# Retention input projection: seven block products in place of eight

## The chip, the cores and the metric

The kernel runs on one core of a Trainium2 chip. The metric is device time in microseconds. All arithmetic is float32; a float32 product is made of three matmuls on halves (a high part rounded to TensorE's fast float32 format and a low rest): high x high, low x high, high x low.

## The reference, cut to what matters

A trunk of two layers on 1024 tokens of width 1024: retention and an MLP, then chunked attention and an MLP. The change touches the first step, the projection of the normed input `hn` by the combined weight of retention (1024 x 6144: q 1024, k 1024, v 2048, gate 2048), and what is done at once with its four parts:

```python
hn = x * rsqrt(mean(x * x) + EPS) * mix_norm_g
proj = hn @ w_in                       # (1024, 6144)
q, k, v, g = split(proj)               # 4 heads: q, k 256 wide, v, g 512 wide
q, k = rope(q, pos), rope(k, pos) * RET_DK ** -0.5
# rope: t1*cos - t2*sin, t1*sin + t2*cos, for the two halves of 128 of each head
o = chunkwise retention of q, k, v with decay per head; then GroupNorm per head
y = silu(g) * o
h = x + y @ w_out
```

## The kernel before, in words

Engines: PE multiplies, DVE and ACT split and scale, POOL adds, SP issues most DMAs. The residual `h` lies transposed in SBUF: eight blocks `h[m]` of 128 features by 1024 tokens, worked on in two halves of 512 tokens (`hf`). Each token's 1/rms is kept as a row `rB`, equal on all partitions, and as columns `rcol`; it is applied after the products, which therefore start before the norm is known. `class Norm` (L185) makes the split operands of all sixteen (m, hf) pieces (`operand`) and the square sums (`square`, `sums`, `turn`).

The projection (L599 to L740) multiplies block by block. `xload` reads x in eight pieces of 512 KB, `xturn` turns each block by PE into PSUM, and operands and `h` are made from PSUM. `up_group` (L439) makes one PSUM bank of 128 columns by 512 tokens from 8 blocks x 3 matmuls. Queries and keys come in pairs of such banks: the rope (L644) takes four products by DVE and two adds by POOL with the tables `cosr`, `sinr` in SBUF, scaled once by `rB` (`rope_scale`), and stores to `qS`, `kS` in DRAM. The first group is multiplied while the second half of x is still being turned (L673 to L680). Values are made with tokens on partitions (`proj_tok`, L451: operands of x as weights, eight banks at once), scaled by ACT with `vsc` (decay times 1/rms) and stored to `vS`; the first half of head 0 stays in SBUF, already split (L703). Then the first queries and keys are loaded and split (L722 to L727), and the gate groups run: DVE scales, ACT does the SiLU, DVE the gain, and the store goes to `gS` (L728 to L740). Weights come 512 KB at a time (`wload`, two buffers) and are split by ACT and DVE.

The core of retention (L742) takes heads in turn: `score`, `turn_k`, `state`, `outs`, `gate`, with q, k, v and gate reloaded from DRAM through rings, and the output projection as filling work.

The other three large projections (both MLPs, attention input) already run a scheme with seven block products for eight (`XNorm` L266, `Group` L324, `Seven` L353). It is Strassen's scheme in Winograd's form: x is cut into 2 x 2 (even or odd feature blocks by token halves), the weight of 256 columns into 2 x 2 (even or odd feature blocks by column halves), and products 1, 2, 5, 6, 3, 7, 4 of four blocks x 3 matmuls are added into three PSUM banks A, B, C. Operands 1, 2 and 5, 6 (`EARLY`) are made before the stage, 3, 7, 4 (`late`) during it; `Group.sums` makes the weight sums on DVE, `make` splits a weight two products ahead (`AHEAD`). After product 2, 3, 7 and 4 one of the four results is complete, and the job's `done(z, hf, src)` finishes it (z: column half). The first two groups are interleaved, so that the late operands have time. Weights come 1 MB per group.

What sets the order: the program is built ahead of time; each engine and each DMA queue works through its own fixed list, which follows the program's order but lets later work whose inputs are expected move ahead. Tiles of one tag share `bufs` places; a new tile waits for the release of an old one, also where a closed pool's place is used again.

Of the kernel before, what the change touches and what calls it, by code (L numbers as in the profile page):

```python
# [76 lines left out]
def trunk_kernel(ctx: ExitStack, tc: tile.TileContext, I, out):  # L77
# [64 lines left out]
    plain = {}  # L142
# [25 lines left out]
    def tmp_tile(pl, name, dt=F32):  # L168
        return pl.tile([P, HT], dt, name=name, tag="tmp", bufs=9 if pl is plain.get("gp") else 5)
# [96 lines left out]
    class XNorm(Norm):  # L266
# [18 lines left out]
        def block(self, m, hf):  # L285
# [3 lines left out]
            if self.seen[j] < 4:  # L289
                return  # L290
# [3 lines left out]
            x.split(1, j, b11)  # L294
            nc.vector.scalar_tensor_tensor(out=t1, in0=b[0][1], scalar=g[0], in1=b11, op0=ALU.mult, op1=ALU.subtract)
            x.scaled(2, j, b[1][0], g[1])
# [4 lines left out]
        def late(self, xb):  # L301

            x, gp = self.x, self.gp
            x.add(xb, LATE)
# [19 lines left out]
    class Group:  # L324
# [9 lines left out]
        def sums(self, ws, products):  # L334
            a = self.a
            for p in products:
                self.s[p] = t = ws.tile([P, 4, P], F32, name="wS", tag="wS", bufs=4)
# [15 lines left out]
    class Seven:  # L353
# [4 lines left out]
        AHEAD, NORM = 2, 4  # L358

        def __init__(self, wa, jobs):  # L360
            self.wa, self.jobs, self.groups = wa, jobs, {}
            self.steps = ([(i, p) for i in range(2) for p in EARLY] + [(0, 3), (1, 3), (0, 7), (0, 4), (1, 7), (1, 4)]
                          + [(i, p) for i in range(2, len(jobs)) for p in SEVEN])
# [11 lines left out]
        def ready(self, s):  # L375
# [3 lines left out]
            if s == 0:  # L379
# [16 lines left out]
        def go(self, wr, psp, gp, x, hooks):  # L396
# [3 lines left out]
            for s, (i, p) in enumerate(self.steps):  # L400
# [20 lines left out]
                if s >= self.NORM:  # L421
# [4 lines left out]
    def spread(norm, xb, psp, more=()):  # L426
# [3 lines left out]
        for hf in range(2):  # L430
            hooks[2].append(lambda hf=hf: norm.sums(psp, hf))
            hooks[Seven.NORM].append(lambda hf=hf: norm.turn(psp, hf))
# [166 lines left out]
    rs = ctx.enter_context(ExitStack())  # L599
    rq = ctx.enter_context(ExitStack())  # L600
    plain["wp"] = pool(rs, "weightsR", RIGHT)
    with ExitStack() as ph:
        gp = pool(ph, "gemmA", LEFT)
        psp = pool(ph, "psA", None, 8, PSUM)
        norm = Norm(0, gp)
        with ExitStack() as st:
            rp = pool(st, "rope", RIGHT)
            xp = pool(st, "xin", RIGHT)
            cosr = rp.tile([P, S], F32, name="cosr")
            sinr = rp.tile([P, S], F32, name="sinr")  # L610

            def qk_src(i):
                hd, which = i // 2, i % 2
                c0 = which * D + hd * DK
                return [w_in[:, c0 + z * P:c0 + (z + 1) * P] for z in range(2)]

            def xload(hf, between=None):
                xs = []
                for c in range(4):
                    if c == 1 and between:  # L620
                        between()
                    xt = xp.tile([P, 4, 256], F32, name="xt", tag="xt", bufs=4)
                    DMA.dma_start(out=xt, in_=I["x"][0, hf * HT:(hf + 1) * HT, c * 256:(c + 1) * 256].rearrange("(t p) c -> p t c", p=P))
                    xs.append(xt)
                return xs

            def xturn(xs, hf, ms):
                for m in ms:
                    ps = psp.tile([P, HT], F32, name="ps", tag="ps")
                    for t in range(4):  # L630
                        nc.tensor.transpose(ps[:, t * P:(t + 1) * P], xs[m // 2][:, t, (m % 2) * P:(m % 2 + 1) * P], ident)
                    norm.operand(m, hf, ps)
# [5 lines left out]

            def rope_scale(hf):
                sl = slice(hf * HT, (hf + 1) * HT)  # L640
                for tb in (cosr, sinr):
                    nc.gpsimd.tensor_tensor(out=tb[:, sl], in0=tb[:, sl], in1=rB[:, sl], op=ALU.mult)

            def rope(i, hf, p1, p2):  # L644
                hd, dst = i // 2, (qS, kS)[i % 2]
                sl = slice(hf * HT, (hf + 1) * HT)
                a, b, c, d = (rp.tile([P, HT], F32, name=n, tag=n, bufs=2) for n in ("ra", "rb", "rc", "rd"))
                nc.vector.tensor_tensor(out=a, in0=p1, in1=cosr[:, sl], op=ALU.mult)
                nc.vector.tensor_tensor(out=b, in0=p2, in1=sinr[:, sl], op=ALU.mult)
                nc.vector.tensor_tensor(out=c, in0=p1, in1=sinr[:, sl], op=ALU.mult)  # L650
                nc.vector.tensor_tensor(out=d, in0=p2, in1=cosr[:, sl], op=ALU.mult)
                nc.gpsimd.tensor_tensor(out=a, in0=a, in1=b, op=ALU.subtract)
                nc.gpsimd.tensor_tensor(out=c, in0=c, in1=d, op=ALU.add)
                for d, t in enumerate((a, c)):
                    DMA.dma_start(out=dst[hd][d, :, sl], in_=t)

            turns = []
            xs0 = xload(0, lambda: turns.append(load_gains(psp, rp, [I["mix_norm_g"].rearrange("i (b p) -> (i b) p", p=P)], 0)))
            turns.pop()()
            raws = [wload(src, NB, P) for src in qk_src(0)]  # L660
            xs1 = xload(1)
            DMA.dma_start(out=cosr, in_=I["cos"])
            DMA.dma_start(out=sinr, in_=I["sin"])
            DMA.dma_start(out=odec, in_=I["odec"])
            DMA.dma_start(out=odec2, in_=I["odec2"])
            rest = load_gains(psp, rp, [I["mlp_norm_g"].rearrange("i (b p) -> (i b) p", p=P),
                                        I["final_norm_g"].rearrange("(b p) -> b p", p=P),
                                        I["ret_gn_g"][0].rearrange("(b p) -> b p", p=P)], 2 * NB)
            xturn(xs0, 0, range(4))
            ws = [wsplit(raws[0], NB, P, "act", "pool")]  # L670
            xturn(xs0, 0, range(4, NB))
            ws.append(wsplit(raws[1], NB, P, "act", "dve"))
            first = {0: [up_group(psp, norm, ws[0], 0)]}  # L673
            xturn(xs1, 1, range(NB))
# [3 lines left out]
            first[0].append(up_group(psp, norm, ws[1], 0))  # L678
            rest()
            first[1] = [up_group(psp, norm, w, 1) for w in ws]  # L680
            norm.sums(psp, 0)
            norm.sums(psp, 1)
            for i in range(1, 2 * RH):
                ws = [wunit(src, NB, P) for src in qk_src(i)]
                for hf in range(2):
                    p1, p2 = (up_group(psp, norm, w, hf) for w in ws)
                    if i == 1:
                        norm.turn(psp, hf)
                        rope_scale(hf)
                        rope(0, hf, *first[hf])  # L690
                    rope(i, hf, p1, p2)

        vdec = gp.tile([P, NB, RH], F32, name="vdec")
        DMA.dma_start(out=vdec, in_=I["vdec"])
        vsc = gp.tile([P, NB, RH], F32, name="vsc")
        for i in range(RH):
            nc.vector.tensor_tensor(out=vsc[:, :, i], in0=vdec[:, :, i], in1=rcol, op=ALU.mult)
        yp = pool(rs, "yR", RIGHT)
        vv = {}
        v0 = [yp.tile([P, 4, HT], F32R, name=n, tag=n, bufs=2) for n in ("yh", "yl")]  # L700
        for hd in range(RH):
            def evac(t, ps, hd=hd):
                if hd == 0 and t < 4:  # L703
                    hi, lo = vv[0, t] = tuple(z[:, t, :] for z in v0)
                    sc = vsc[:, t, 0:1]
                    nc.scalar.activation(hi, ps, AF.Copy, scale=sc)
                    nc.vector.scalar_tensor_tensor(out=lo, in0=ps, scalar=sc, in1=hi.bitcast(F32), op0=ALU.mult, op1=ALU.subtract)
                    return
                vt = tmp_tile(gp, "t")
                nc.scalar.activation(vt, ps, AF.Copy, scale=vsc[:, t, hd:hd + 1])  # L710
                DMA.dma_start(out=vS[hd][t * P:(t + 1) * P, :], in_=vt)
            proj_tok(psp, norm, w_in[:, 2 * D + hd * DV:2 * D + (hd + 1) * DV], evac)

        cq = pool(rq, "coreRqk", RIGHT)
        qk, kt, sc, stt = {}, {}, {}, {}
        maskt = cq.tile([P, RH, P], F32, name="maskt")
        DMA.dma_start(out=maskt, in_=I["mask"])

        def qk_tiles():
            return [cq.tile([P, 2, HT], F32R, name=n, tag=n, bufs=3) for n in ("qkh", "qkl")]  # L720

        for nm, src in (("q", qS), ("k", kS)):  # L722
            qk[0, nm, 0] = qk_tiles()
            for d in range(2):
                raw = tmp_tile(gp, "raw0")
                DMA.dma_start(out=raw, in_=src[0][d, :, 0:HT])
                split(raw, *(t[:, d, :] for t in qk[0, nm, 0]))  # L727
        def gate_evac(m, hf, ps):  # L728
            sl = slice(hf * HT, (hf + 1) * HT)
            t = tmp_tile(gp, "t")  # L730
# [588 lines left out]
```

## Time and profile before

| | us |
|---|---|
| runs | 2832.45, 2836.87, 2838.62 |
| median | 2836.87 |
| profiled execution | 2835.71 |
| its span, first to last instruction | 2833.9 |
| PE / DVE / ACT / POOL busy | 2751.2 / 1655.6 / 1080.2 / 170.2 |
| HBM read / written | 221.59 / 89.69 MB |

Busy time is the union of an engine's instructions. Matmuls are pipelined, so an instruction's duration is longer than the distance to the next; the distance is the price. The granted clock of PE has two levels, 1.2 and 2.4 GHz, and 1.00 means the higher one throughout. The projection takes the first fifth of the span; the MLPs' and the attention's projections lie at 895, 1563 and about 2150 us.

### The profile page before, as it was taken

To read this page: it belongs to the slowest core of one execution; us is meant where nothing else is said; L and a number is where in the kernel's file an instruction comes from. 1 tells how busy PE (TensorE), PEld (TensorE's weight loads), DVE (VectorE), ACT (ScalarE), POOL (GpSimd) and SP (SyncE) were. 2 spreads that over 40 slices of the span, in tenths; PEclk is the share of its full clock that TensorE was granted. 3 is DMA by queue.
4 is the path that set the end of the run, shared out by engine and by line. 5 is a ranking of instruction groups with operands and counts; after the bars stand their busy time and mean duration, and the time that the engine had idled before them with its cause. 6 is when DMAs were issued, how large, how long until landed. Compare 5 with 4: busy or idle time off the path is not lost.

```text
span 2833.9 us, 34421 instructions
## 1 busy us (share of the span) xinstructions
PE 2751.2 (97%) x12762; PEld 2262.3 (80%) x12762; DVE 1655.6 (58%) x2969; ACT 1080.2 (38%) x1930; POOL 170.2 (6%) x235
## 2 busy tenths in 40 slices
PE   8999999999999999999999999789989999999998
PEld 7888888878887788878888788578877888788887
DVE  5431123366658756554446867599988665644445
ACT  4001222243326444432123534387775444412222
POOL 1320000000000000000000000233320000000000
PEclk9999999999999999999999999899999999999999
DMA  4321333353210333252331455765512333433321
GB/s 146 105 96 60 112 107 98 99 172 112 82 60 27 117 114 110 93 169 89 97 100 45 113 193 156 198 166 151 151 50 71 104 110 114 147 96 99 112 86 60
DMA packets 246648, 310.92 MB, mean 110 GB/s; under 512 B 14568, under 2 KB 172368, under 8 KB 244432
## 3 DMA queue, kind: packets, MB, share of 16 engines
q1 hardware_dynamic: 244816, 304.46, 34.5%
q0 software_dynamic: 1536, 4.20, 0.5%
q8 instruction: 100, 1.64, 0.2%
q14 instruction: 68, 0.56, 0.1%
q10 hardware_dynamic: 128, 0.06, 0.0%
HBM read 221.59 MB, written 89.69 MB: 110 GB/s over the span
## 4 chain that ended last, share of the span: by engine, by line
PE 85%; DVE 8%; ACT 3%; DMA 2%; issue 1%; SPq 0%; POOL 0%; DVEq 0%; ACTq 0%
PE ps L166 18%; PE ps L164 18%; PE ps L165 18%; PE pA L164 6%; PE pA L166 5%; PE pA L165 5%; PE pC L164 3%; PE pC L166 3%; PE pC L165 3%; DVE pr L1151 1%; DVE ptl L140 1%; PE pB L164 1%; PE pB L166 1%; PE pB L165 1%; PE po L1187 1%
## 5 line engine op out<-in xcount | busy, mean ns | idle before, releaser
L491 DVE TENSOR_TENSOR h<-ps,h 128x512 f32<-128x512 f32 x352 | 242.4, 689 | 339.4 <-PE ps L166 338.9
L136 ACT CAST whi<-wraw 128x1024 fp32r<-128x1024 f32 x132 | 139.0, 1053 | 769.9 <-PE ps L165 601.6
L165 PE MATMUL ps<-ul,whi 128*128 128x512 f32 x960 | 374.0, 390 | 1.9 <-DVE ul L140 1.7
L166 PE MATMUL ps<-uh,wlo 128*128 128x512 f32 x960 | 373.5, 389 | 0.0
L164 PE MATMUL ps<-uh,whi 128*128 128x512 f32 x960 | 373.0, 389 | 0.0
L166 PE MATMUL pA<-xh,wl 128*128 128x512 f32 x704 | 277.2, 395 | 10.0 <-DVE wl L140 10.0
L164 PE MATMUL pA<-xh,wh 128*128 128x512 f32 x704 | 278.3, 400 | 3.4 <-DVE c L417 2.7
L165 PE MATMUL pA<-xl,wh 128*128 128x512 f32 x704 | 278.2, 395 | 0.0
L140 DVE TENSOR_TENSOR wlo<-wraw,whi 128x1024 fp32r<-128x1024 f32 x131 | 165.0, 1260 | 165.4 <-ACT whi L136 165.3
L165 PEld LDWEIGHTS ps<-ul,whi 128*128 128x128 f32 x960 | 180.2, 188 | 41.2 <-DVE ul L140 3.6
L164 PEld LDWEIGHTS ps<-uh,whi 128*128 128x128 f32 x960 | 180.1, 188 | 37.6 <-ACT uh L136 0.4
L166 PEld LDWEIGHTS ps<-uh,wlo 128*128 128x128 f32 x960 | 180.2, 188 | 37.1
L164 PE MATMUL ps<-hhi,whi 128*128 128x512 f32 x512 | 202.8, 396 | 2.2 <-ACT whi L136 1.4
L165 PE MATMUL ps<-hlo,whi 128*128 128x512 f32 x512 | 202.3, 395 | 0.0
L166 PE MATMUL ps<-hhi,wlo 128*128 128x512 f32 x512 | 202.3, 395 | 0.0
L164 PEld LDWEIGHTS pA<-xh,wh 128*128 128x128 f32 x704 | 133.4, 190 | 43.2 <-DVE c L417 13.6
L166 PEld LDWEIGHTS pA<-xh,wl 128*128 128x128 f32 x704 | 133.6, 190 | 41.2 <-DVE wl L140 12.7
L165 PEld LDWEIGHTS pA<-xl,wh 128*128 128x128 f32 x704 | 133.5, 190 | 27.1
L136 ACT CAST wh<-wS 128x512 fp32r<-128x512 f32 x176 | 109.0, 621 | 116.0 <-PE pB L165 59.1
L164 PE MATMUL pC<-xh,wh 128*128 128x512 f32 x352 | 139.1, 395 | 3.3 <-ACT wh L136 2.1
L166 PE MATMUL pC<-xh,wl 128*128 128x512 f32 x352 | 138.6, 394 | 1.0 <-DVE wl L140 1.0
L165 PE MATMUL pC<-xl,wh 128*128 128x512 f32 x352 | 138.6, 394 | 0.0
(243 smaller groups left out, 5528.0 us busy)
## 6 DMA issues: line engine op xcount, KB each, us to landing
wr<-in_mlp_w_dram SPq DMA_DIRECT2D x32, 1024.0 KB, 5.4
uD<-c SPq DMA_DIRECT2D x128, 256.0 KB, 2.0
wraw<-in_mlp_w_dram SPq DMA_DIRECT2D x64, 512.0 KB, 3.4
xr<-uD SPq DMA_DIRECT2D x128, 256.0 KB, 3.1
wraw<-in_ret_w_in_dram SPq DMA_DIRECT2D x48, 512.0 KB, 4.1
kk<-kA SPq DMA_DIRECT2D x32, 512.0 KB, 8.1
wr<-in_att_w_in_dram SPq DMA_DIRECT2D x12, 1024.0 KB, 5.3
gS<-t SPq DMA_DIRECT2D x32, 256.0 KB, 4.1
```

Source lines behind the costliest of these rows:

```text
L136: nc.scalar.copy(out=hi, in_=src)
L140: eng.tensor_tensor(out=lo, in0=src, in1=hi.bitcast(F32), op=ALU.subtract)
L164: nc.tensor.matmul(ps, lhsT=lh, rhs=rh, start=start, stop=False, skip_group_check=more)
L165: nc.tensor.matmul(ps, lhsT=lh, rhs=rl, start=False, stop=False, skip_group_check=more)
L166: nc.tensor.matmul(ps, lhsT=ll, rhs=rh, start=False, stop=stop, skip_group_check=more)
L491: nc.vector.tensor_tensor(out=hv, in0=ps, in1=hv, op=ALU.add)
L1151: nc.vector.tensor_tensor_reduce(out=pr[:, :w].rearrange("p (a b) -> p a b", a=nh), in0=ps[:, 0:nh, :hw], in1=bt[:, 640 - w:640].rearrange ...
L1187: nc.tensor.matmul(po[:, oc:oc + n], lhsT=T[hd, "v"][:, kb, :], rhs=t[:, off[kb]:off[kb] + n], start=i == 0, stop=i == len(seq) - 1)
```

## The change

The projection is given to `Seven`, with 24 jobs in place of the query, key, value and gate loops. Values now come out with features on partitions and are turned by PE (`v_group`). The rope tables are scaled by `rB` once, written to DRAM (`cD`) and loaded again by each of the eight rope groups; the rope runs on DVE alone. `xturn` stores x to `h` first and makes operands 1 and 2 from it when the first half is there, 5 and 6 (`early`) with the second. The first two groups' list of products is split after two (`heads=2`), results wait until product 6 (`norm=6`). Queries and keys of head 0 are loaded and split behind the last gate group, and the first values of head 0 go through DRAM like all others. All operands and first weights lie to the right in SBUF, where the core's tiles follow. Removed: `Norm.operand` for this stage, `qk_src`, `rope`, `rope_scale`, `up_group` and `proj_tok` calls, and the gate loop (shown above). The core of the diff:

```diff
-    plain = {}
+    plain = {"bufs": 9}
...
         def __init__(self, gain, gp, xa, xt, bufs):       # XNorm
-            self.fresh = lambda: xt.tile([P, HT], F32, name="xr", tag="xr", bufs=bufs)
+            self.fresh = lambda: xt.tile([P, HT], F32, name="xr", tag="xr", bufs=bufs) if xt else tmp_tile(gp, "xr")
...
+            if self.seen[j] == 4:
+                self.early(j)
+        def early(self, j, raw=True):
...
             nc.scalar.activation(b11, b[0][0], AF.Copy, scale=g[0])
+            if raw:
+                x.split(1, j, b11)
             nc.vector.scalar_tensor_tensor(out=t1, in0=b[0][1], scalar=g[0], in1=b11, op0=ALU.mult, op1=ALU.subtract)
+            if raw:
+                x.scaled(2, j, b[1][0], g[1])
             x.split(5, j, t1)
...
-            x.add(xb, LATE)
+            x.add(xb, (4, 7, 3))
...
+        def __init__(self, wa, jobs, heads=4, norm=4):    # Seven
+            self.steps = ([(i, p) for i in range(2) for p in EARLY[:heads]] + [(i, p) for i in range(2) for p in EARLY[heads:]] if heads < 4
+                          else [(i, p) for i in range(2) for p in EARLY])
+            self.steps = (self.steps + [(0, 3), (1, 3), (0, 7), (0, 4), (1, 7), (1, 4)]
...
-                if s >= self.NORM:
+                if s >= self.norm:
...
+    cD = [dram.tile([2, P, HT], F32, name=f"cD{i}") for i in range(2)]
+    plain.update(bufs=11, wS=3)
...
+    def v_group(i):
+        hd = i // 2
+        def done(z, hf, src):
+            t = src
+            if z == 1 and hf == 0:
+                t = tmp_tile(gp, "c")
+                nc.vector.tensor_copy(out=t, in_=src)
+            pv = psp.tile([P, 4, P], F32, name="pv", tag="ps")
+            vt = tmp_tile(gp, "vt").rearrange("p (t f) -> p t f", t=4)
+            for y in range(4):
+                nc.tensor.transpose(pv[:, y, :], t[:, y * P:(y + 1) * P], ident)
+            for y in range(4):
+                nc.scalar.activation(vt[:, y, :], pv[:, y, :], AF.Copy, scale=vsc[:, 4 * hf + y, hd:hd + 1])
+            c0 = (i % 2) * 2 * P + z * P
+            DMA.dma_start(out=vS[hd][hf * HT:(hf + 1) * HT, c0:c0 + P].rearrange("(t p) c -> p t c", p=P), in_=vt)
...
+    def gate_group(i):
+        def done(z, hf, src):
...                                                       # as gate_evac
+            (nc.gpsimd if i == 7 else DMA).dma_start(out=gS[m // 4][(m % 4) * P:(m % 4 + 1) * P, sl], in_=t)
...
+    def rope_group(which, hd):
+        have, tab = {}, {}
+        def tables(hf):
+            tab[hf] = [tmp_tile(gp, n) for n in ("cos", "sin")]
+            for t, src in zip(tab[hf], cD):
+                DMA.dma_start(out=t, in_=src[hf])
+        def done(z, hf, src):
+            have[z, hf] = src
+            if (z, hf) == (0, 1):
+                tables(1)
+            if z == 0:
+                return
+            p1, p2, (cs, sn) = have[0, hf], src, tab[hf]
+            a, b = tmp_tile(gp, "ra"), tmp_tile(gp, "rb")
+            nc.vector.tensor_tensor(out=a, in0=p1, in1=cs, op=ALU.mult)
+            nc.vector.tensor_tensor(out=b, in0=p2, in1=sn, op=ALU.mult)
+            nc.vector.tensor_tensor(out=a, in0=a, in1=b, op=ALU.subtract)
+            nc.vector.tensor_tensor(out=p1, in0=p1, in1=sn, op=ALU.mult)
+            nc.vector.tensor_tensor(out=b, in0=p2, in1=cs, op=ALU.mult)
+            nc.vector.tensor_tensor(out=b, in0=b, in1=p1, op=ALU.add)
+            for d, t in enumerate((a, b)):
+                DMA.dma_start(out=(qS, kS)[which][hd][d, :, hf * HT:(hf + 1) * HT], in_=t)
+            if hf == 1:
+                tables(0)
...
+    jobs = [v_group(0), v_group(1)]
+    for hd in range(RH):
+        jobs += [rope_group(0, hd)] + ([v_group(2 * hd + 2)] if hd < 3 else []) + [rope_group(1, hd)] + ([v_group(2 * hd + 3)] if hd < 3 else [])
+    jobs += [gate_group(i) for i in range(8)]
+    seven = Seven(pool(xs, "wsevenAA", RIGHT), jobs, heads=2, norm=6)
...
+        psp = pool(ph, "psA", None, 2, PSUM)
+        norm = XNorm(0, gp, xa, None, 0)
...
             def xturn(ts, hf):
+                for m in range(NB):
+                    ps = psp.tile([P, HT], F32, name="px", tag=("ps", "A", "B", "C")[m % 4])
...                                                       # 4 transposes, then h[m] from ps by ACT (odd m) or DVE
+                    if hf == 0:
+                        norm.x.scaled(1 + m % 2, m // 2, hv, gains[:, 0, m:m + 1])
+                    elif m % 2:
+                        norm.early(m // 2, raw=False)
...
+            seven.begin()
+            x1 = xload(1)
...
+            xturn(x0, 0)
+            xturn(x1, 1)
+            rest()
             for hf in range(2):
                 for m in range(NB):
                     norm.square(m, hf)
+        def scales():
+            DMA.dma_start(out=vdec, in_=I["vdec"])
...                                                       # vsc; then for both tables and halves:
+                    t = tmp_tile(gp, "tab")
+                    DMA.dma_start(out=t, in_=src[:, sl])
+                    nc.vector.tensor_tensor(out=t, in0=t, in1=rB[:, sl], op=ALU.mult)
+                    DMA.dma_start(out=dst[hf], in_=t)
...
+        seven.go(wr, psp, gp, norm.x, spread(norm, xb, psp, [(6, scales)], 4, 6))
+    xs.close()
...
+    for nm, src in (("q", qS), ("k", kS)):
+        qk[0, nm, 0] = qk_tiles()
+        for d in range(2):
+            raw = tmp_tile(gp, "raw0")
+            DMA.dma_start(out=raw, in_=src[0][d, :, 0:HT])
+            split(raw, *(t[:, d, :] for t in qk[0, nm, 0]))
...
-            items = [it for it in items if it[:2] != (0, 0)]
+            items = [it for it in items if it not in ((0, 0, "q"), (0, 0, "k"))]
...
-                if hd:
-                    take(hd, 0, "v0")
-                    take(hd, 0, "v1")
+                take(hd, 0, "v0")
+                take(hd, 0, "v1")
```

## Rows read from the trace of the kernel before

**Rows 1.** The page, part 1: busy us (share of the span) xinstructions.

```profile
PE 2751.2 (97%) x12762; PEld 2262.3 (80%) x12762; DVE 1655.6 (58%) x2969; ACT 1080.2 (38%) x1930; POOL 170.2 (6%) x235
```

**Rows 2.** Windows: from:to, length, busy (xcount) by engine, clock, DMA share, GB/s.

```profile
13.73:560.70 546.97, 544.66 (x2361) 438.20 (x2362) 166.17 (x229) 118.69 (x165) 55.58 (x37) 1.00 0.30 98
560.70:584.10 23.40, 18.30 (x95) 15.19 (x94) 16.64 (x37) 14.42 (x22) 0.00 (x0) 0.94 0.82 285
```

**Rows 3.** Groups by line, 0 to 562 us, PE: busy us, mean ns | idle before.

```profile
L164 PE MATMUL ps<-hhi,whi 128*128 128x512 f32 x512 | 202.8, 396 | 2.2 <-ACT whi L136 1.4 <-ACT h L635 0.8
...
L164 PE MATMUL ps<-whi,hhi 128*128 128x512 f32 x256 | 101.2, 396 | 0.0
```

**Rows 4.** Timeline of PE at the projection's end: start us, us, instruction.

```profile
547.64 0.40 PE L165 MATMUL ps<-hlo,whi 128*128 128x512 f32 x1
...
560.70 0.40 PE L164 MATMUL ps<-qkh 128*128 128x512 f32 x1
```

**Rows 5.** Timeline of SP: weight loads of the first MLP (12) and the attention.

```profile
956.19 0.38 SPq L330 DMA_DIRECT2D wr<-in_mlp_w_dram  x1
...
1167.77 0.38 SPq L330 DMA_DIRECT2D wr<-in_mlp_w_dram  x1
...
1648.61 0.38 SPq L330 DMA_DIRECT2D wr<-in_att_w_in_dram  x1
...
1712.00 0.38 SPq L330 DMA_DIRECT2D wr<-in_att_w_in_dram  x1
...
1770.38 0.37 SPq L330 DMA_DIRECT2D wr<-in_att_w_in_dram  x1
```

**Rows 6.** Timeline of DVE in the attention projection's first groups.

```profile
1592.85 0.75 DVE L319 SCALAR_TENSOR_TENSOR t<-h,gall,xh 128x512 f32<-128x512 f32 x1
1593.51 0.68 DVE L140 TENSOR_TENSOR wl<-wS,wh 128x512 fp32r<-128x512 f32 x1
1594.11 0.69 DVE L320 TENSOR_TENSOR t<-t,xl 128x512 f32<-128x512 f32 x1
```

**Rows 7.** The page, part 5: ACT's casts of weight sums.

```profile
L136 ACT CAST wh<-wS 128x512 fp32r<-128x512 f32 x176 | 109.0, 621 | 116.0 <-PE pB L165 59.1
```

**Rows 8.** Windows of the attention projection's start.

```profile
1560.00:1600.00 40.00, 38.28 (x175) 30.07 (x173) 36.97 (x68) 26.16 (x53) 0.00 (x0) 1.00 0.20 53
1600.00:1620.00 20.00, 16.61 (x60) 12.73 (x61) 16.62 (x28) 7.27 (x13) 0.00 (x0) 0.83 0.73 210
```

**Rows 9.** Timeline of DVE and ACT at the kernel's start.

```profile
4.83 0.17 DVE L123 COPY gall<-pg 128x16 f32<-128x16 f32 x1 [3.44 <-PE pg L122]
...
12.63 1.04 ACT L136 CAST whi<-wraw 128x1024 fp32r<-128x1024 f32 x1 [2.12 <-DMA wraw<-in_ret_w_in_dram]
```

**Rows 10.** Timeline of PE in the attention projection's first groups.

```profile
1603.39 0.80 PE L166 MATMUL pA<-xh,wl 128*128 128x512 f32 x1 [3.43 <-DVE wl L140]
...
1608.35 0.60 PE L165 MATMUL pA<-xl,wh 128*128 128x512 f32 x1
1608.78 0.41 PE L166 MATMUL pA<-xh,wl 128*128 128x512 f32 x1
```

**Rows 11.** Timeline of PE between the attention's projection and its core.

```profile
1817.41 0.39 PE L166 MATMUL pA<-xh,wl 128*128 128x512 f32 x1
1829.53 0.45 PE L1146 MATMUL pS<-kk,qh 128*128 128x128 f32 x1 [11.73 <-DMA qh<-qA]
```

**Rows 12.** Timeline of SP there.

```profile
1817.87 1.10 SPq L1072 DMA_DIRECT2D qh<-qA  x2
```

**Rows 13.** The page, part 6: DMA issues, KB each, us to landing.

```profile
wr<-in_mlp_w_dram SPq DMA_DIRECT2D x32, 1024.0 KB, 5.4
...
xr<-uD SPq DMA_DIRECT2D x128, 256.0 KB, 3.1
```

**Rows 14.** Tile c in the attention projection: landing of its stores.

```profile
DMA to landing us min/median/max: 2.2/2.4/11.2
```

More of the change, by code (lines that the diff above doesn't have):

```diff
@@ L168, in tmp_tile @@
     def tmp_tile(pl, name, dt=F32):
-        return pl.tile([P, HT], dt, name=name, tag="tmp", bufs=9 if pl is plain.get("gp") else 5)
+        return pl.tile([P, HT], dt, name=name, tag="tmp", bufs=plain["bufs"] if pl is plain.get("gp") else 5)
     def rsqrt_newton(sd, v, y):
@@ L353, in trunk_kernel @@
     class Seven:
[L358 to L362, printed above, removed]
+        AHEAD = 2
+        def __init__(self, wa, jobs, heads=4, norm=4):
+            self.wa, self.jobs, self.groups, self.norm = wa, jobs, {}, norm
+            self.steps = ([(i, p) for i in range(2) for p in EARLY[:heads]] + [(i, p) for i in range(2) for p in EARLY[heads:]] if heads < 4
+                          else [(i, p) for i in range(2) for p in EARLY])
+            self.steps = (self.steps + [(0, 3), (1, 3), (0, 7), (0, 4), (1, 7), (1, 4)]
                           + [(i, p) for i in range(2, len(jobs)) for p in SEVEN])
@@ L424, in go, with spread @@
                     pending.clear()
-    def spread(norm, xb, psp, more=()):
+    def spread(norm, xb, psp, more=(), sums=2, turn=4):
         gen = norm.late(xb)
@@ L430, in spread @@
         for hf in range(2):
-            hooks[2].append(lambda hf=hf: norm.sums(psp, hf))
-            hooks[Seven.NORM].append(lambda hf=hf: norm.turn(psp, hf))
+            hooks[sums].append(lambda hf=hf: norm.sums(psp, hf))
+            hooks[turn].append(lambda hf=hf: norm.turn(psp, hf))
         for i in range(12):
@@ new lines, in rope_group @@
+    def rope_group(which, hd):
[22 more added lines that the diff above has]
+                tables(0)
+        c0 = which * D + hd * DK
+        return w_in[:, c0:c0 + DK], done
@@ L606, in trunk_kernel @@
         with ExitStack() as st:
[L607 to L615, printed above, removed]
+            xp = pool(st, "xin", LEFT)
             def xload(hf, between=None):
-                xs = []
+                ts = []
@@ L657, in trunk_kernel @@
             turns = []
-            xs0 = xload(0, lambda: turns.append(load_gains(psp, rp, [I["mix_norm_g"].rearrange("i (b p) -> (i b) p", p=P)], 0)))
+            x0 = xload(0, lambda: turns.append(load_gains(psp, xp, [I["mix_norm_g"].rearrange("i (b p) -> (i b) p", p=P)], 0)))
             turns.pop()()
[L660 to L663, printed above, removed]
@@ L677, in trunk_kernel @@
                     norm.square(m, hf)
[L678 to L684, printed above, removed]
-                for hf in range(2):
[L686 to L727, printed above, removed]
@@ L742, in trunk_kernel @@
+    maskt = cq.tile([P, RH, P], F32, name="maskt")
+    DMA.dma_start(out=maskt, in_=I["mask"])
+    gs.close()
+    plain.update(bufs=9, wS=4)
     with ExitStack() as ph:
```

97 lines of the change are left out of this document (40 added, 57 removed).

## The prediction

> **What bounds it now.** I read the page's engine shares first: PE is busy for 97% of the span [rows 1], so a change pays only through work taken off PE or pauses put on it. Then the windows of the stage that the diff rewrites: between its first product at 13.73 us and the first score of the core at 560.70, PE is busy 544.66 of 546.97 us, DVE 166, ACT 119, DMA engines 30% [rows 2]. The groups by line give what PE does there: 512 and 256 triples, 768 x 3 = 2304 matmuls of 128x512 [rows 3]. In PE's timeline the 56 matmuls from 547.64 to 560.70 start 0.233 us apart, and the core's first one follows the last of the projection without a gap [rows 4]: the stage is PE alone, and its end has no slack, so what it loses or gains there the end of the kernel loses or gains, if the core behind it is fed as early.
>
> **The parts.** *Products.* 24 groups of 256 columns with 7 products of 12 matmuls are 2016, 288 fewer. I price them by whole groups from the stages that run `Seven` now, by the distance of their weight loads on SP [rows 5]: MLP groups (1167.77 - 956.19) / 11 = 19.235 us; query and key groups of the attention (1770.38 - 1712.00) / 3 = 19.46; its value groups, with the same 16 transposes by PE as the new `v_group`, (1712.00 - 1648.61) / 3 = 21.13. The new list has 8 value, 8 rope and 8 gate groups. Those behind the first two cost 6 x 21.13 + 8 x 19.46 + 8 x 19.235 = 436.4 us if PE stays the bound.
>
> Does it? On DVE a 128x512 operation of two tensors follows the one before after 0.60 us, one with a scale after 0.66 [rows 6]. A rope group has 4 weight sums, 7 low halves, 3 block sums and 12 rope operations, 26 x 0.60 = 15.6 us under PE's 19.46; the rope's adds came from POOL before and are in this count. A gate group has 22 (13.2 us), a value group 15 (9.0). ACT in a value group: 10 of 128x512 and 16 of 128x128; even at the price of a 128x512 cast, 0.621 us [rows 7], 26 x 0.621 = 16.1 of 21.13. All fit, so these engines cost nothing here but through their order.
>
> *The start* is where I expect to lose. Before, a group of products could begin with half of x and 0.5 MB of weights. Now operands 1 and 2 need the first half, 5 and 6 the second, and 3, 7, 4 more passes, while the norm's squares, weight sums and splits want the same DVE. Up to the last product of the first two groups DVE has at 0.60: 8 copies from PSUM, 8 low halves of operands 5 and 6, 14 square sums, 14 weight low halves, 8 weight sums, 12 steps of operands 7 and 4, 6 block sums, 70 x 0.60 = 42.0; at 0.66: 8 for operands 1 and 2, 8 for the two differences, 12 for operands 3, 7 and 4, 28 x 0.66 = 18.5; with ten short ones of the norm some 62 us. In the nearest stretch, the first two groups of the attention, DVE was busy 36.97 of 40 us [rows 8], 92%, which makes 67. DVE's first work comes at 5 us, and in the trace of before ACT waited for weights until 12.63 us [rows 9], with 2.5 MB come by then; the new first piece is 1 MB behind the same 2 MB, so by the same rate about 15. The half of x that DVE can treat meanwhile is 4 x 0.60 + 8 x 0.66 = 7.7 us: I charge 5 us of waiting. The two groups end at 5 + 5 + 67 = 77 us. The bounds: 67 with DVE dense and never waiting; 90 at 80% and 8 us of waiting. PE needs only 2 x 21.13 = 42.3 of this, so it pauses in pieces, as it does in the attention's start (3.43 us for a low weight half [rows 10]).
>
> So the last product ends at 77 + 436.4 = 513.4 against 560.70.
>
> *The seam.* Query, key and mask of head 0 were loaded, and the first values split, long before; now the query and key loads stand behind the last gate group, in tiles that lie where the last weights were, and the first values come from DRAM. The nearest seam of this kind is the attention's: SP issued the query at 1817.87, only behind other loads, and PE stood from 1817.41 to 1829.53, 11.7 us of waiting [rows 11, 12]. Below it is bounded by nothing, as before. Here the early operands' space comes free three to seven products (8 us and more) ahead, the scores and turns of the core (some 5 us) come before the first values are wanted, and SP is less loaded; I take 5, between the two.
>
> *Tables.* Each rope group loads four tables of 256 KB, once scaled by 1/rms and kept in DRAM. Like reloads of the MLP land in 3.1 us, a weight block in 5.4 [rows 13]. They depend on nothing but a free tile, of which there are 11, and I count nine in use at the worst moment. DVE would wait behind a late table, and the low weight halves with it, but these are made two products (5.5 us) ahead. I take 3 us for the eight groups together; below 0, above see the slower rival. The scaling itself (4 operations, 2 MB of traffic) lies in groups 2 and 3, the stores and gates where they did, the last group's on POOL's queue, which has nothing else.
>
> **The sum.** The core starts at 513.4 + 5 + 3 = 521.4, 39.3 us sooner. The profiled execution took 2835.71 us; 2835.71 - 39.3 = 2796. It lies 1.2 us under the median of the three runs, so I let 2796 stand for either.
>
> **A rule that speaks against it.** In the attention's start, after the pause of 3.43 us, matmuls went 0.43 us apart, the lower level (1.2 GHz), until 1608.78 [rows 10], with a granted clock of 0.83 over that window [rows 8]: some 13 matmuls x 0.2 = 2.6 us. My sum contains no such drop. The Trainium skill, "TensorE: Matmul & The Clock Gate", section "HAM oscillation — how this bites in real kernels", says that a kernel whose PE pauses for its inputs again and again pays the slow restart each time; the trace shows it once there. By that rule the longer start here would pay it at each of some four pauses, 4 x 2.6 = 10 us more, 2806.
>
> **Rivals.** (a) *The seam becomes the attention's*: 11.7 us and a slow restart of 2.6 instead of 5, and the start takes its upper half, say 3 more: 2808. For it: head 0's tiles overlay live space. Against: few loads stand ahead. (b) *The clock* as just told: 2806. (c) *A dense start and a closed seam*: DVE ends its list at 70, the seam costs 1, the tables nothing: 2796 - 7 - 4 - 3 = 2782. For it: PE's queue is fed by independent work. (d) *Slower: the tables come late.* A weight block is issued in every group just when the first-half tables are. If a table landed as late as the slowest store of the block sums in the attention stage, 11.2 us [rows 14], issued one product (2.7) before its use, DVE would stand 8.5 us, 3.0 beyond the lead of 5.5. In 16 halves that is 48 us: 2796 + 48 = 2844, and the saving is gone from 8.0 us of waiting in each half on. Against it: DMA engines are at 30% here [rows 2], and the median of those stores is 2.4 us [rows 14]. (e) *Seven for eight saves less than its count*, since its groups run at DVE's pace: this needs more than 19.46 us of DVE in a rope group, 15.6 counted.
>
> **How the numbers follow.** Forecast 0.56, its own range 2787 to 2805 (start -6 to +7, seam -4 to +3, tables -3 to +4, not all together); (a) 0.14, (b) 0.08, (c) 0.12, (d) with (e) 0.06, and 0.04 for a small gain within 10 us, by several of these at once. A measurement of this kernel can tell about 0.2% (5.7 us) from no change. Faster by more: 0.91; within it 0.03; slower 0.06. The range for 8 in 10 takes in most of (a), (b) and (c): 2781 to 2814.
>
> **What would show it.** Group distances of 19.2 to 19.5 and 21.1 us in the weight loads and the last product near 513 us. The first two groups ending by 77 with PE's waits put down to DVE's operands (wrong if to DMA of x or weights). A wait of the first score or the first state product for head 0's loads of about 5 us. PE waits in rope groups under 0.5 us each; (d) would show DVE waiting for the tables there and PE for low weight halves. No less than 2781 unless the start never starves PE, no more than 2830 unless a wait repeats in every group.

## The result, and the profile after

The changed kernel takes 2819.44 us (median of four runs, 2814.55 to 2820.22) against 2837.57 (four runs, 2832.45 to 2838.62): a ratio of 0.9936, 95% interval 0.9924 to 0.9948. That is 18 us faster, where 41 were forecast; the direction was right, and the size lies outside the range. In what follows, what the changed kernel gains is told against the kernel before, and what a run gains against the changed kernel, as a difference of medians. By the ratios, each taken with its own runs of the kernel before, these gains differ by up to 2.4 us, and the intervals reach 3 to 6 us to either side: what is smaller than that rests on the traces and not on the times.

The profiled execution took 2819.48 us, its span is 2817.4. Part 1 of the page, the line that answers to [rows 1]:

```profile
PE 2712.9 (96%) x12602; PEld 2228.5 (79%) x12602; DVE 1853.7 (66%) x3332; ACT 1197.6 (43%) x2240; POOL 117.4 (4%) x202
```

PE has 38 us less to do than before, and the kernel gained 16.5 of them in its span. Two windows of the new start say where part of the rest is (from:to, length, then busy time and count of PE, PEld, DVE, ACT, POOL; granted clock, DMA share, GB/s):

```profile
20.00:40.00 20.00, 12.57 (x50) 9.37 (x48) 20.00 (x33) 20.00 (x39) 0.00 (x0) 0.76 0.09 24
40.00:60.00 20.00, 17.11 (x66) 12.99 (x65) 16.75 (x32) 10.90 (x20) 0.00 (x0) 0.81 0.00 1
```

From 20 to 40 us DVE and ACT are full, DMA is idle, PE is at 12.57 of 20. PE's timeline there, with what ended each wait:

```profile
27.28 0.39 PE L165 MATMUL pA<-xl,wh 128*128 128x512 f32 x1
29.57 0.47 PE L164 MATMUL pB<-xh,wh 128*128 128x512 f32 x1 [1.90 <-DVE h L707]
35.81 0.79 PE L166 MATMUL pA<-xh,wl 128*128 128x512 f32 x1 [5.54 <-DVE wl L140]
36.40 0.63 PE L164 MATMUL pA<-xh,wh 128*128 128x512 f32 x1
36.83 0.63 PE L165 MATMUL pA<-xl,wh 128*128 128x512 f32 x1
...
46.88 1.21 PE L223 MATMUL pc<-ones,acc 128*128 128x2 f32 x8 [1.77 <-DVE acc L212]
48.14 0.79 PE L164 MATMUL pC<-xh,wh 128*128 128x512 f32 x1
```

Every wait in this stretch is for DVE; behind it the longest is one of 1.7 us for ACT, and ahead of 20 us PE waits 3.6 us for x. Behind two of the waits the distance of matmuls goes to 0.43 us (36.40 to 36.83, and again from 48.14 to 54.21), the lower level of the clock. DVE's timeline at the end of its list for the first two groups, and PE's first matmul of the third group's second product:

```profile
78.28 0.70 DVE L140 TENSOR_TENSOR wl<-wr,wh 128x512 fp32r<-128x512 f32 x1
90.79 0.69 DVE L622 COPY c<-pA 128x512 f32<-128x512 f32 x1 [3.86 <-PE pA L166]
```

```profile
92.33 0.40 PE L164 MATMUL pB<-xh,wh 128*128 128x512 f32 x1
```

The last low half that these groups need is done at 79.0. PE ends them at 90.75, which releases DVE's copy at 90.79, and the third group's second product begins at 92.33.

From 95 us to the last product PE waits once, for 0.9 us. The weight loads on SP, which answer to [rows 5] (query or key and value groups in turn, then gate groups):

```profile
101.88 0.37 SPq L334 DMA_DIRECT2D wr<-in_ret_w_in_dram  x1
121.82 0.38 SPq L334 DMA_DIRECT2D wr<-in_ret_w_in_dram  x1
142.83 0.37 SPq L334 DMA_DIRECT2D wr<-in_ret_w_in_dram  x1
...
464.57 0.38 SPq L334 DMA_DIRECT2D wr<-in_ret_w_in_dram  x1
484.06 0.38 SPq L334 DMA_DIRECT2D wr<-in_ret_w_in_dram  x1
```

A pair takes 40.95 us (142.83 - 101.88), a gate group 19.49. The last product starts its last matmul at 531.00. Then the seam, on PE and on SP; [rows 11, 12] show the attention's:

```profile
531.00 0.39 PE L166 MATMUL pA<-xh,wl 128*128 128x512 f32 x1
539.99 0.79 PE L164 MATMUL ps<-qkh 128*128 128x512 f32 x1 [8.59 <-ACT qkh L136]
```

```profile
518.89 10.91 SPq L147 DMA_DIRECT2D wraw<-in_ret_w_out_dram  x4
530.57 1.06 SPq L760 DMA_DIRECT2D raw<-qS  x2
```

Four loads of the output weights, which nobody needs yet, stand on SP in front of head 0's queries and keys; the fourth waits for a split until 529. The core starts at 539.99 instead of 560.70, 20.7 us sooner, and from there 4 of these are lost until the end.

### The profile page after: what moved, and what is told of

Same layout as the page of the kernel before. It is cut to its first block, busy times and chain, and to the rows that moved or that the text cites. A ratio compares the mean times of both kernels' runs of the same rounds, so it can differ in the third digit from the quotient of the medians.

```text
span 2817.4 us, 34988 instructions
## 1 busy us (share of the span) xinstructions
PE 2712.9 (96%) x12602; PEld 2228.5 (79%) x12602; DVE 1853.7 (66%) x3332; ACT 1197.6 (43%) x2240; POOL 117.4 (4%) x202
## 4 chain that ended last, share of the span: by engine, by line
PE 82%; DVE 10%; ACT 4%; DMA 2%; issue 2%; SPq 0%; POOL 0%; DVEq 0%; ACTq 0%
PE ps L165 12%; PE ps L164 12%; PE ps L166 12%; PE pA L164 9%; PE pA L166 8%; PE pA L165 8%; PE pC L164 4%; PE pC L166 4%; PE pC L165 4%; PE pB L164 2%; PE pB L165 2%; PE pB L166 2%; DVE pr L1175 2%; DVE ptl L140 1%; ACT pr L1179 1%
## 5 line engine op out<-in xcount | busy, mean ns | idle before, releaser
L166 PE MATMUL pA<-xh,wl 128*128 128x512 f32 x1088 | 429.2, 396 | 15.1 <-DVE wl L140 15.1
L164 PE MATMUL pA<-xh,wh 128*128 128x512 f32 x1088 | 433.2, 402 | 5.5 <-DVE c L423 3.6
L165 PE MATMUL pA<-xl,wh 128*128 128x512 f32 x1088 | 431.5, 397 | 0.0
L136 ACT CAST wh<-wr 128x512 fp32r<-128x512 f32 x204 | 126.8, 623 | 232.6 <-PE pA L165 119.8
L140 DVE TENSOR_TENSOR wl<-wS,wh 128x512 fp32r<-128x512 f32 x272 | 186.4, 688 | 51.5 <-ACT wh L136 50.0
L164 PE MATMUL pC<-xh,wh 128*128 128x512 f32 x544 | 216.6, 398 | 3.9 <-ACT wh L136 2.0
L166 PE MATMUL pC<-xh,wl 128*128 128x512 f32 x544 | 216.6, 399 | 1.5 <-DVE wl L140 1.5
L165 PE MATMUL pC<-xl,wh 128*128 128x512 f32 x544 | 216.0, 397 | 0.0
L140 DVE TENSOR_TENSOR wl<-wr,wh 128x512 fp32r<-128x512 f32 x204 | 139.7, 687 | 72.5 <-ACT wh L136 72.4
L542 ACT ACTIVATE c<-c 128x512 f32<-128x512 f32 x128 | 81.2, 634 | 148.0 <-DVE c L541 145.1
```

What stands on the lines that cost most here:

```text
L136: nc.scalar.copy(out=hi, in_=src)
L140: eng.tensor_tensor(out=lo, in0=src, in1=hi.bitcast(F32), op=ALU.subtract)
L164: nc.tensor.matmul(ps, lhsT=lh, rhs=rh, start=start, stop=False, skip_group_check=more)
L165: nc.tensor.matmul(ps, lhsT=lh, rhs=rl, start=False, stop=False, skip_group_check=more)
L166: nc.tensor.matmul(ps, lhsT=ll, rhs=rh, start=False, stop=stop, skip_group_check=more)
L542: nc.scalar.activation(t, t, AF.Square)
```

## The experiments

**Is it DVE?** n1 leaves 12 of the 14 adds of the square sums out of the start, those of blocks 1 to 6 in both halves, so that the first norm is not the true one (the expectation counts 14 and 8.4 us; 12 are 7.2 us at 0.60):

```diff
                 nc.scalar.activation(sq, hv, AF.Square)
-                nc.vector.tensor_tensor(out=self.acc[hf], in0=self.acc[hf], in1=sq, op=ALU.add)
+                if not (self.gain == 0 and m < 7):
+                    nc.vector.tensor_tensor(out=self.acc[hf], in0=self.acc[hf], in1=sq, op=ALU.add)
```

> Leaves out 14 of the 14 adds on DVE (0.60 us each, 8.4 us) that sum the squares for the first norm except the last block's, so most of the norm is missing; the squares themselves stay on ACT. Theory DVE: the first two groups end at about 90 us because DVE has more in that stretch than PE, so they end 6 to 8.4 us sooner and the whole gets 6 to 8 us faster than the changed kernel. Rival clock: the two stretches at half clock (36.4 to 41 and 48.1 to 54.2 us) set the end, and they stay or move: less than 3 us. Rival ACT: ACT is as full as DVE from 20 to 40 us, so relief of DVE alone gives less than 3 us.

2811.61 us, ratio 0.9909 (0.9890 to 0.9927), 8 us faster. In n1 DVE's last low half starts 9.0 us sooner than in the changed kernel, and the third group's second product 8.9 us sooner, for 7.2 us of DVE:

```profile
69.31 0.69 DVE L140 TENSOR_TENSOR wl<-wr,wh 128x512 fp32r<-128x512 f32 x1
```

```profile
83.46 0.40 PE L164 MATMUL pB<-xh,wh 128*128 128x512 f32 x1
```

ACT has as many squares and splits as before, so it is not ACT's length that sets the end. One of the two slow stretches went with the waits (granted clock 1.00 from 40 to 60 us), so this alone does not part DVE from the clock. How far two executions of one start lie apart is seen in n2 and w2 below, which change nothing ahead of the seam: there the third group's second product begins at 91.24 and 91.25, 1.1 us sooner than in the changed kernel.

**One weight half earlier.** n4 puts the split that PE misses at 27 us in front of the turning of x:

```diff
-            seven.begin()
+            seven.wr = wr
+            seven.begin(3)
```

> The split of group 1's first weight block is put into the list before the turning of x, one step earlier than in the changed kernel. Theory order: the 8.5 us hole of PE from 27.3 to 35.8 us, waiting for that block's low half, is lost time of its own: PE goes on at 27 us, and the first two groups end 5 to 8 us sooner. Theory DVE: the hole only moves, since DVE's list stays as long: the two groups end within 2 us of 90 us.

2822.51 us, 0.9952 (0.9937 to 0.9967): not faster. PE's waits by what ended them, n4, 5 to 100 us:

```profile
PE px L705 <- DMA xt<-in_x_dram: 6.5, 2, 6.1
PE pB L166 <- DVE wl L140: 5.0, 1, 5.0
PE pc L223 <- DVE acc L212: 4.1, 2, 3.2
```

The hole has moved on to the next low half, to the sums and ahead of x. The third group's second product begins at 91.15, no sooner than in n2 and w2. The edit moves more than the split: the load of that group's weights now stands on SP in front of the second half of x (issued by 7.4 us instead of at 14.68), and PE's longest wait for x is 6.1 us instead of 2.2. So n4 does not test the order by itself.

**Is it the clock?** w1 fills PE's waits with 52 matmuls that nobody reads:

```diff
+                if self.norm == 6 and s in (1, 2, 3):
+                    warm = psp.tile([P, HT], F32, name="warm", tag="ps")
+                    for _ in range((0, 32, 12, 8)[s]):
+                        nc.tensor.matmul(warm, lhsT=wh[:, 0, :], rhs=x.hi[1][:, 0, :], start=True, stop=True)
```

> 52 matmuls more, on operands that are there and into a bank that nobody reads, at the places in PE's list where it waits in the start (before the second weight low half of group 1, and before the norm's sums). DVE's list stays. Theory clock: PE then keeps 2.4 GHz; the two stretches at half clock (36.4 to 41, 48.1 to 54.2 us) vanish, product 6 of group 0 begins at about 51 us instead of 53.8 and the two groups end 3 to 5 us sooner. Theory DVE alone: the clock costs nothing, since what PE waits for comes at DVE's pace, and the groups end within 1 us of 92 us.

2821.26 us, 0.9938 (0.9924 to 0.9951): no change. The windows of w1:

```profile
20.00:40.00 20.00, 20.00 (x92) 16.56 (x91) 20.00 (x34) 20.00 (x38) 0.00 (x0) 0.98 0.07 20
40.00:60.00 20.00, 18.57 (x82) 14.64 (x82) 17.88 (x36) 11.94 (x23) 0.00 (x0) 0.91 0.01 2
```

The first slow stretch is gone, the second is shortened (granted clock 0.98 and 0.91, in the changed kernel 0.76 and 0.81), and the third group's second product comes at 91.04, 1.3 us sooner. That is hardly more than the 1.1 of n2 and w2, whose start is not filled. Eight matmuls still go at the lower pace (47.95 to 51.47), 0.2 us too slow each, so at most some 1.6 us more could be had from the clock. What sets the end is DVE.

**Length or order of DVE's list?** d1 leaves nothing out and makes squares and sums later:

```diff
-            for hf in range(2):
-                for m in range(NB):
-                    norm.square(m, hf)
+        hooks = spread(norm, xb, psp, [(8, scales)], 6, 8)
+        for s, hf, ms in [(3, 0, [0, 1, 2, 3, 4, 5, 6, 7]), (4, 1, [0, 1, 2, 3, 4, 5, 6, 7])]:
+            hooks[s].insert(0, lambda hf=hf, ms=ms: squares(hf, ms))
```

(with `norm=8` and 12 temporary tiles).

> Nothing is left out: the 16 squares, their 14 adds and what follows of the norm come later in the program (squares behind products 3 and 4 of the list, sums behind product 6, results wait until product 8, one more temporary tile). DVE has as much to do, but the low halves and operands of products 1 to 6 of both groups no longer stand behind the adds. Theory order on DVE: PE gets its inputs 6 to 8 us sooner while DVE's list ends where it did (79 us), what PE has left behind it shrinks, and the two groups end 5 to 8 us sooner, as in n1. Theory length of DVE's list alone: the end stays at 79 plus PE's rest, within 2 us.

2814.78 us, 0.9920 (0.9907 to 0.9933). DVE's last low half for the two groups is done at 78.7 us, in the changed kernel at 79.0; the weight load at 101.88 moves to 99.97. That is 1.9 us, but 0.8 against n2 and w2 (100.78, 100.76): the order gives little, and the length counts. The whole is 4.7 us faster, but the intervals of the two kernels overlap.

**Can POOL take it?** p1 gives all 14 adds to POOL, p2 those of the first half:

```diff
-                nc.vector.tensor_tensor(out=self.acc[hf], ...)
+                (nc.gpsimd if self.gain == 0 else nc.vector).tensor_tensor(out=self.acc[hf], ...)
```

> All 14 adds of the first norm's square sums go to POOL, which has nothing else then; an add of this size took POOL 1.3 us in the kernel before, so 14 make 18 us from about 33 us on. Theory DVE: 8.4 us less on DVE, the two groups end up to 8 us sooner as in n1, but PE's fixed list has the 8 small matmuls of the sums right behind product 2 and waits there for POOL until about 52 us: what comes of it is 2 to 6 us. Rival (DVE's length is not what counts, n1 was faster for having no sums to wait for): no gain or a loss of up to 5 us.

> Only the 7 adds of the first token half go to POOL (9 us from about 33 us on), those of the second stay on DVE. Theory DVE: 4.2 us less on DVE and no long wait for the sums: the two groups end 3 to 5 us sooner than in the changed kernel, the whole as much. Rival: within 1.5 us.

p1 2827.71 us, 0.9963 (0.9950 to 0.9976), 8 us slower than the changed kernel; p2 2822.11, 0.9950 (0.9934 to 0.9967), no gain. In p1, the waits of PE, the adds on POOL (line, shapes, count, busy, mean ns; they run from 33.04 to 55.91 us), one group of DVE's operations from 33 to 55 us, then DVE's timeline:

```profile
PE pc L223 <- POOL acc L212: 12.1, 2, 8.5
```

```profile
L212 POOL TENSOR_TENSOR acc<-acc,sq 128x512 f32<-128x512 f32 x14 | 21.9, 1569 | 32.7 <-DVE xl L140 31.7
```

```profile
L264 DVE SCALAR_TENSOR_TENSOR xl<-h,gall,xh 128x512 fp32r<-128x512 f32 x4 | 6.9, 1773 | 0.0
```

```profile
37.57 1.76 DVE L140 TENSOR_TENSOR wl<-wr,wh 128x512 fp32r<-128x512 f32 x1
57.87 0.16 DVE L182 TENSOR_SCALAR vc<-pc 128x4 f32<-128x4 f32 x1 [8.44 <-PE pc L223]
85.41 0.69 DVE L140 TENSOR_TENSOR wl<-wr,wh 128x512 fp32r<-128x512 f32 x1
```

The same two operations take 748 and 691 ns in the changed kernel. While POOL adds, eight of DVE's ten operations on two tensors of SBUF take 1.65 to 1.77 us, some 2.4 times as long (the first of the ten 0.69, the last 1.08); one that reads PSUM and SBUF (L423, at 47.75) takes 0.68 as ever. That is some 8 us more for them, so what was moved came back; both theories had missed that. Then DVE stands 8.44 us for the norm's sums, for which PE waits until POOL is through: about what p1 lost. The Trainium skill, "SBUF — State Buffer", section "Who interferes with whom", says that the two engines contend for one pair of ports; these rows agree.

DVE's last low half starts 7.1 us later than in the changed kernel, and the third group's second product begins at 99.90, 7.6 us later. So in n1, the changed kernel and p1 the last low half starts at 69.31, 78.28 and 85.41 and that product at 83.46, 92.33 and 99.90, each time 14.0 to 14.5 us behind: the end of DVE's list moves the end of the start one for one.

**The seam.** n2 loads head 0's queries, keys and the mask from POOL's queue, and stores the last gate group from SP's:

```diff
-            DMA.dma_start(out=raw, in_=src[0][d, :, 0:HT])
+            nc.gpsimd.dma_start(out=raw, in_=src[0][d, :, 0:HT])
```

> Head 0's first queries and keys and the mask are loaded from POOL's queue instead of SP's, and the last gate group's stores go from SP's. Theory queue: the loads stood on SP behind the fourth load of the output weights, which waits for a split on DVE until 529.4 us; on an empty queue they start some 5 to 8 us sooner and the 8.6 us pause before the core's first score falls to 0 to 4, with the half clock behind it: 5 to 10 us faster than the changed kernel. Rival space: the loads wait for their places (temporary tiles, operands' space) until about 530 us whatever the queue: the pause stays at 7 to 9, within 2 us.

2811.07 us, 0.9915 (0.9900 to 0.9930), 8 us faster, 6 by the ratios. POOL's and PE's timelines in n2:

```profile
513.80 1.19 POOL L760 DMA_DIRECT2D raw<-qS  x2
515.05 0.54 POOL L760 DMA_DIRECT2D raw<-kS  x1
517.99 0.77 POOL L760 DMA_DIRECT2D raw<-kS  x1 [2.41 <-DMA gS<-c]
```

```profile
534.15 0.50 PE L164 MATMUL ps<-qkh 128*128 128x512 f32 x1 [3.00 <-ACT qkh L136]
```

The same loads start 17 us sooner: not their places held them, but the queue (only the fourth waits for a place, 2.41 us). The pause falls from 8.59 to 3.00, and the core starts at 534.15, 5.8 us sooner than in the changed kernel, 5.6 of them from the pause. The 3.00 that are left are no load's any more: ACT's casts of the queries and keys stand in its list behind the last gate group's SiLU at 531.92:

```profile
532.46 2.17 ACT L136 CAST qkh<-raw 128x512 fp32r<-128x512 f32 x4
```


**Steady groups.** In the changed kernel the matmuls of one group do not all go at one pace. PE's timeline in a gate group, the first pair from product 6, the second from product 3:

```profile
480.17 0.39 PE L165 MATMUL pA<-xl,wh 128*128 128x512 f32 x1
480.39 0.39 PE L166 MATMUL pA<-xh,wl 128*128 128x512 f32 x1
...
482.66 0.40 PE L164 MATMUL pC<-xh,wh 128*128 128x512 f32 x1
482.89 0.39 PE L165 MATMUL pC<-xl,wh 128*128 128x512 f32 x1
```

Over twelve, the distance is 0.2264 us in products 1, 2, 5 and 6, and 0.234 in 3, 7 and 4, without a wait and at full clock. The operands of 3, 7 and 4 lie at the left end of SBUF (`xlateA`), all others and the split weights at the right. n3 moves them; m1 exchanges early and late ones:

```diff
-        xb = pool(ph, "xlateA", LEFT)
+        xb = pool(ph, "xlateA", RIGHT)        # n3 and m1
-    xa = pool(xs, "xearlyA", RIGHT)
+    xa = pool(xs, "xearlyA", LEFT)            # m1
```

> The operands of products 3, 7 and 4 are placed at the right end of SBUF, where the other operands and the split weights of this stage lie, instead of at the left end. All engines' lists are the same. In the changed kernel matmuls of products 1, 2, 5 and 6 go 0.2264 us apart and those of 3, 7 and 4 go 0.234 apart, in the MLPs (all to the left) all go 0.2264 apart. Theory place: a matmul is 3% slower when its moving operand and its weights lie at opposite ends, so 36 x 0.0075 = 0.27 us per group and 22 groups make 5 to 6 us: gate groups at 19.2 us instead of 19.48, the whole 4 to 6 us faster than the changed kernel. Rival operand: the data of the late operands or DVE's traffic sets it: 0.234 stays and the time is the same within 2 us.

> The early operands at the left end of SBUF and the late ones at the right end, with the split weights at the right: the exchange of what the changed kernel has. Theory place: now products 1, 2, 5 and 6 go 0.234 us a matmul and 3 and 7 go 0.2264. Rival, that it hangs on the late operands or their tile as such: 0.2264 for 1, 2, 5 and 6.

n3 2814.89 us, 0.9924 (0.9909 to 0.9939), 4.5 us faster; m1 2822.44, 0.9948 (0.9927 to 0.9968); the intervals of both overlap with the changed kernel's, and the paces decide. In m1 the two paces have changed sides (PE's timeline in a gate group, first product 5, then product 7):

```profile
481.52 0.40 PE L164 MATMUL pC<-xh,wh 128*128 128x512 f32 x1
481.76 0.40 PE L165 MATMUL pC<-xl,wh 128*128 128x512 f32 x1
...
488.48 0.39 PE L164 MATMUL pA<-xh,wh 128*128 128x512 f32 x1
488.71 0.39 PE L165 MATMUL pA<-xl,wh 128*128 128x512 f32 x1
```

Product 5, its operand now at the left, goes 0.24 apart (0.2345 over twelve); product 7, now at the right, 0.2264 over twelve. In the MLP's groups, where everything lies at the left, the distance is 0.2264 too (four products in a row, before, 1004 to 1015 us). So the place decides, and neither end is slow by itself: 3% more where the two operands of a matmul lie at opposite ends. In n3 a pair of groups takes 40.6 us and a gate group 19.33, 3 us less over the stage.

**Together.** c1 is n2 with n3, c2 adds p2, d2 is c1 with d1.

> The seam's loads on POOL's queue (n2) and the late operands at the right end (n3) together. If the two gains have different causes they add up: 8 and 4.5 make 12 to 13 us, about 2807 us. If both only shifted the same chance (the clock at the seam or in the MLP's start): 8 us, about 2811.

> The same with the first half's adds on POOL as well. Theory DVE: another 3 to 5 us, about 2803 us, the last product some 4 us sooner than in c1. Rival: as c1.

> The same with the seam's loads on POOL's queue and the late operands at the right end. By theory order 2803 to 2806 us; by theory length as c1, about 2811.

c1 2811.42 us, 0.9911 (0.9896 to 0.9926); c2 2810.65, 0.9907 (0.9892 to 0.9922); d2 2807.95, 0.9893 (0.9878 to 0.9909), the fastest: 11.5 us under the changed kernel, 29 under before. What c2 was to add did not come: its core starts at 534.77, 5.9 us later than c1's, and it takes no longer. d2's core starts only 0.8 us sooner than c1's, so most of the 3.5 us between them arose behind it and proves nothing for the order. In c1 the core starts 11.1 us sooner than in the changed kernel and 5.2 sooner than in n2, but its span ends with n2's (2806.8 and 2806.7). Of the 5.2 there are 4.3 left in the first MLP's groups (weight loads at 928.10 and 932.44), 2.7 in the attention's (1744.60 and 1747.27), none at the end. What lies between is the first MLP's start and the later ones, with the same instructions in both. Windows of the MLP's start, in n2 and then in c1:

```profile
880.00:890.00 10.00, 9.96 (x46) 7.94 (x45) 8.97 (x24) 6.87 (x15) 0.00 (x0) 1.00 0.06 22
910.00:920.00 10.00, 9.56 (x34) 7.46 (x35) 6.84 (x12) 3.21 (x6) 0.00 (x0) 0.83 0.87 281
```

```profile
870.00:880.00 10.00, 9.55 (x43) 7.71 (x42) 7.42 (x20) 3.93 (x9) 0.00 (x0) 0.83 0.36 104
900.00:910.00 10.00, 6.94 (x21) 5.21 (x20) 7.33 (x13) 2.92 (x5) 0.00 (x0) 0.71 0.66 194
```

The granted clock falls there in one and less in the other; in the second MLP's start (2120 to 2160 us) it is 0.91 and 0.92 in c1 and 1.00 in n2. Over the whole it was 0.984 in c1 and 0.987 in n2. That the clock takes the gain back is read from such windows; no run holds the clock in the later stages, so it is not shown.

**Fillings that failed.** w2 puts 120 small matmuls on `ones` into the seam of the changed kernel; w3 is c1 with w1 and 50 of them.

```diff
+        warm = psp.tile([P, HT], F32, name="warm", tag="ps")
+        for _ in range(120):
+            nc.tensor.matmul(warm[:, :P], lhsT=ones, rhs=ones, start=True, stop=True)
```

> 120 small matmuls of 128x128 into a bank that nobody reads, between the last product and the core's first score, which waits there for 8.6 us. Theory clock: the scores then run at 0.23 us for 512 columns instead of 0.43, and the core's first products come 2 to 3.5 us sooner; as much is gained at the end, if the first MLP's start has the same clock. Rival: the core's start is paced by DVE and ACT (masks, splits of the scores), so nothing is gained.

> Queue of the seam's loads, place of the late operands, and both fillings (50 small matmuls at the seam) in one kernel. If each gives what it gave alone: 8 and 4.5 and 3 to 8, about 2803 us. If what is gained before the core is lost again to the clock in the starts of the later stages, as in the kernel with the first two (granted clock 0.984 over the whole against 0.987 with the queue alone): 2808 to 2811 us.

w2 2828.76 us, 0.9970 (0.9959 to 0.9982), 9 us slower; w3 2816.53, 0.9922 (0.9908 to 0.9935), 5 slower than c1. PE in w2:

```profile
530.03 12.84 PE L747 MATMUL warm<-ones 128*128 128x128 f32 x114
543.02 0.47 PE L164 MATMUL ps<-qkh 128*128 128x512 f32 x1
560.61 0.80 PE L164 MATMUL ps<-vh,kth 128*128 128x512 f32 x1 [11.82 <-ACT kth L829]
```

The 114 of them behind the last product took 0.113 us each, 12.84 in all, more than the pause. The scores then run 0.23 apart, as theory clock has it. But the builder, with the filling in its plan, put loads and splits of later values ahead of the scores' splits on SP, ACT and DVE, and PE stood 11.8 us behind them. In w3 the same wait is 5.11 us. What the slow clock at the seam costs stays open.

## Why the prediction was wrong

**Products**: right. PE is the bound from the third group on, waiting 0.9 us in all. The groups behind the first two took 440.6 us (from 90.75 to 531.39) against 436.4. The price was taken from the attention, whose query groups (19.46) had the slow products in them unseen, and from the MLP (19.235), which has none: gate groups cost 19.49. n3 brings 3 of the 4 us.

**The start**: this is the step that failed, "The two groups end at 5 + 5 + 67 = 77 us". DVE's list did end near there: 79.0, although it held 2.6 us of the tables' scaling that the count of its operations leaves out. But 77 is the end of DVE's work, and I took it for the end of PE's. Behind the last low half PE still had 32 matmuls of both groups' products and 12 turns of values, with a wait of 1.0 us for an evacuation and 7 matmuls of the third group between them, 11.8 us; 90.75 against 77. n1 and p1 show that the end of DVE's list sets it. My upper bound, 90, came near only by charging DVE with more waiting, not by this rest of PE's. The clock rule that I weighed, 10 us for four pauses, counted the drops fairly: two in the start, one behind the seam, more in later stages. In the start filling the pauses brought 1.3 us (w1), not told apart from the 1.1 between two executions, since PE there waits for DVE anyway.

**The seam**: 8.59 us instead of 5, with the mechanism of rival (a), loads behind other loads. I had written that SP was less loaded there and had not counted the output weights' loads, which the builder moves ahead (n2). The attention's seam, my nearest case, has two such loads (1813.50 us) in front of its query as well.

**Tables**: 3 us charged, nothing measured. They landed in 5.3 to 5.7 us, and DVE waited for them once, 0.6 us. Rival (d) is refuted, and so is (e), as the distances show.

**Behind the core**: I let 39.3 us at the core be 39.3 at the end. Of 20.7 there, 17.5 were left in the first MLP's groups (956.19 in [rows 5] answers to 938.66), 14.1 in the attention's (1648.61 to 1634.53), 16.5 at the end. The change adds no instruction there and takes none out. After, the granted clock is 0.83 and 0.73 in two windows of the MLP's start (880 to 890, 910 to 920 us); it is 1.00 in all of that start before. Why the drops came there is open.

The sum: 13.8 (start) + 4.2 (groups) - 3 (tables) + 3.6 (seam) = 18.6 at the core's start, 4 to 5 behind it: 2796 + 23 = 2819.

## What to carry to other kernels

Where one engine's list sets the pace of a start, add to its end what the next engine still has to do on the last inputs: the end of the list is not the end of the stage. Look at every load that waits behind another on one queue, those of later stages too, which a planning builder moves ahead; a queue that has nothing else gave 6 to 8 us for three changed lines. A saving ahead of unchanged stages is not yet a saving at the end (here 20.7 us became 16.5, and c1's 5.2 over n2 became nothing): compare the stages behind the change as well.

## What had not been expected of the hardware

A matmul of 128x512 goes 0.2264 us after the one before where both operands lie at the same end of SBUF, 0.234 where they lie at opposite ends (n3, m1). While POOL adds two tensors of SBUF, DVE's operations on two such tensors take 1.65 to 1.77 us instead of 0.69 to 0.75 (p1). A 128x128 matmul on `ones` took 0.113 us at full clock, half of a 128x512 one for a quarter of the columns (w2).
